# One core, four sublayers in fp32-by-splitting: half of the last block pair of each FFN computed plainly, and joined high/low activations for wider matmuls

## The chip, the core and the metric

The kernel runs on one core of a Trainium2 chip. Its time is the device time of one execution in microseconds (us), as the median of several runs. TensorE (PE) multiplies, VectorE (DVE) and ScalarE (ACT) prepare and collect operands, GpSimd (POOL) does a few elementwise steps and issues some transfers, and SyncE (SP) issues the weight transfers.

## The reference

The input is 256 tokens of width 2048 in float32. There are two layers. Each has a mixer and a dense FFN, both between RMS norms:

```python
for layer in range(DEPTH):                      # DEPTH = 2
    h = rms_norm(x, g[0])
    # layer 0: proj = h @ even_w_in;  GLA (8 heads) and neighbourhood attention (8 heads)
    # layer 1: proj = h @ odd_w_in;   SSD (16 heads) and sliding-window attention (8 heads)
    mix = concat(o_a, o_b) @ w_out
    x = x + rms_norm(mix, g[1])
    h = rms_norm(x, g[2])
    f = (silu(h @ w_gate) * (h @ w_up)) @ w_down   # hidden width 5632 = 11 blocks of 512
    x = x + rms_norm(f, g[3])
```

All weights are float32 and are read from memory once. The result is float32.

## The kernel before

**Arithmetic.** Every float32 operand is split into a high part (a copy that ACT rounds to the fast fp32r format) and a low part (DVE subtracts the high part from the original). A product of two operands is three matmuls: high by high, high by low, low by high. Weights arrive in halves of 128 x 1024 values (512 KB). `halves` (L179) makes `whi` on ACT (L184) and `wlo` on DVE (L186) of each half. Seven buffers of `whi` and seven of `wlo` rotate.

**Two kinds of projection.** `unit_a` (L198) has the activations stationary and 512 weight columns moving: lines L211 to L213, 512 columns each. `unit_b` (L233) has a weight tile of 128 x 128 stationary and the 256 tokens moving: lines L242 to L244, 256 columns each, 16 steps of three matmuls. The even layer uses `unit_b` for 24 weight chunks (queries and keys of both mixers) and for one narrow chunk of 48 used rows (kind "L"); the odd layer uses it for 12 chunks and for one narrow chunk. Activations after a norm are kept as eight tiles of 4 KB per partition, four `xth` and four `xtl` (L315).

**The FFN.** Ten of the eleven hidden blocks are taken in five pairs. While gate and up of a pair are computed, the down projection of the pair before runs in the background (`quads`, L555), half of the output columns at a time (`p` = 0, 1). One such half multiplies a 2 x 2 block matrix by a 2 x 2 block matrix with seven products instead of eight. That needs sums of weight tiles (`sw`, L567, DVE), sums of activations (`combos`, L528), 14 splits of weights (L184, L186), and ten additions of results into `f` and `fu` (L627). The products are lines L618 to L620 into the tile `sq`. Block 10 (`LONE`) has no partner: its gate and up run while the last pair's `quads` finish, and its down projection ends the FFN with a plain `unit_a` in `post` (L513).

**What sets the order.** The code is written as a main stream of projections. Background generators are advanced by `tick` at a given `rate`. A scheduler then orders the instructions of each engine, ahead of time, and allots tiles from pools. Each engine executes its own list in order. `self.tight` makes `unit_a` alternate between the two token halves after each weight half. At the end of `post`, lines pinned in order interleave the next norm with the last matmuls. There `x`, the residual, is loaded again from memory by POOL's queue (`load_x`, L631), added to the normed result (L413 on DVE, L411 on POOL), and transposed on PE.

**Tiles.** The general pool `s4` has 26 slots of 4 KB per partition. It holds the activations, the weight tiles of `quads`, the mixers' work, `f` and `x`.

Of the kernel before, what the change touches and what calls it, by code (L numbers as in the profile page):

```python
# [18 lines left out]
F32 = mybir.dt.float32  # L19
# [7 lines left out]
P = 128  # L27
# [8 lines left out]
PAIRS = [(0, 1), (2, 3), (4, 5), (6, 7), (8, 9)]  # L36
LONE = 10
# [7 lines left out]
NCHUNK = 298  # L45
NQUAD = 80
AHEAD, SETTLE = 2, 4
LAG = 2
# [43 lines left out]
class Trunk:  # L92
    def __init__(self, tc, dr, out, stage=99):
        self.tc, self.nc, self.dr, self.out, self.stage = tc, tc.nc, dr, out, stage
        self.plan = []
        self.pending = deque()
        self.bg = []
        self.early = deque()
        self.hooks, self.mid = deque(), deque()
        self.lag = 2 * LAG  # L100
        self.nraw = 0
        self.rate, self.width, self.credit = 1.0, 3, 0.0
        self.n = 0
        self.pinned = {}
        self.pinning = ()
        self.ready = deque()
        self.tight = False
        self.splan, self.sraw, self.squeue = [], {}, deque()
# [52 lines left out]
    def chunk(self, kind, name, idx, k0, n0):  # L161

        if self.hooks and len(self.plan) == self.hooks[0][0]:
            self.hooks.popleft()[1]()
        self.plan.append((kind, name, idx, k0, n0))
        while len(self.ready) < 2:
            self.prep()
        n = 2 if kind == "A" else 8
        return [tuple(v.rearrange("p (k n) -> p k n", k=n) for v in self.ready.popleft()) for _ in range(2)]

    def prep(self):

        while len(self.early) < 4 and self.nraw < 2 * NCHUNK:
            self.load_half()
        if not self.early:
            return
        self.ready.append(self.halves(self.early.popleft()))
# [20 lines left out]
    def unit_a(self, chunks, xk, evac):  # L198
# [21 lines left out]
        for ci, (name, idx, k0, n0, kt0) in enumerate(chunks):  # L220
            w = self.chunk("A", name, idx, k0, n0)
            if self.tight:
                for half in range(2):
                    part(0, ci, w, kt0, half)
                    part(1, ci, w, kt0, half)
                continue
# [4 lines left out]
            self.push(*(lambda h=h, ci=ci, w=w, kt0=kt0: part(1, ci, w, kt0, h) for h in range(2)))  # L231

# [72 lines left out]
    def begin_norm(self, li, gi):  # L305

        nc = self.nc
        xt = ([None] * 4, [None] * 4)
# [4 lines left out]
        def piece(t, j, src):  # L313
            if xt[0][j] is None:
                xt[0][j], xt[1][j] = self.slot([P, 4, T], F32R, "xth"), self.slot([P, 4, T], F32R, "xtl")  # L315
# [33 lines left out]
    def post(self, li, gi, nseg, after, f=None):  # L349
# [9 lines left out]

        def seg(mk, xk):  # L360
# [3 lines left out]
            if last:  # L364
                self.x = [[None, None], [None, None]]
                for t in range(2):
                    for j in range(2):
                        self.load_x(t, j, nc.gpsimd)
# [48 lines left out]
            for n in range(4):  # L417
                def evac(t, ps, n=n):
# [13 lines left out]
                    if n == 3 and t == 0:  # L432
# [3 lines left out]
                        self.pinning = ("PE", "DVE")  # L436
                if last and n == 2:
                    self.pinned = {}
                    self.pinning = ("PE",)
                self.unit_a(mk(n), xk, evac)  # L440
# [11 lines left out]
    def ffn(self, li, norm, after):  # L452
# [21 lines left out]
        for pi, pair in enumerate(PAIRS):  # L474
            self.squeue.extend((li, b, n) for p in range(2) for b, n in (
                (pair[0], 2 * p), (pair[0], 2 * p + 1), (pair[1], 2 * p + 1), (pair[1], 2 * p)))
        for pi, pair in enumerate(PAIRS):
# [14 lines left out]
            self.spawn(self.quads(li, pair, self.combos(h), f, pi == 0))  # L492
# [5 lines left out]
        self.rate = 2.0  # L498
        gate_up(LONE, whole)
        while self.bg:  # L500
            self.step()
        for n in range(4):
            u = f[2][:, n // 2 * 512:n // 2 * 512 + 512]
            c = slice(n % 2 * 512, n % 2 * 512 + 512)
            for t in range(2):
                d = f[t][n // 2][:, c]
                if n % 2 == 0 and t:
                    nc.vector.tensor_add(d, d, u)
                if n % 2:
                    nc.vector.tensor_sub(d, d, u)  # L510
        self.tight = False
        seg = self.post(li, 3, 1, after, f[:2])
        seg(lambda n: [("ffn_w_down", li, 512 * LONE, 512 * n, 0)], self.xk(ht))  # L513

# [13 lines left out]
    def combos(self, h):  # L528
# [4 lines left out]
        def put(key, src):  # L533
            o = self.slot([P, 2, 4, P], F32R, "so")
            nc.scalar.copy(o[:, 0], src)
            nc.vector.tensor_sub(o[:, 1], src, o[:, 0].bitcast(F32))  # L536
            out[key] = o
# [14 lines left out]
        put("t3", k)  # L552
        return out

    def quads(self, li, pair, ops, f, first):  # L555
# [4 lines left out]
        for p in range(2):  # L560
# [48 lines left out]
            for key in order:  # L609
                ps = self.mx([P, 512], "sq")  # L610
                x = ops[key]
                for i in range(2):
                    next(ahead, None)
                    wh, wl = (v.rearrange("p (k n) -> p k n", k=2) for v in ready.popleft())
                    for k in range(2):
                        s, e = i == 0 and k == 0, i == 1 and k == 1
                        xh, xl = x[:, 0, 2 * i + k], x[:, 1, 2 * i + k]
# [36 lines left out]
    def setup(self, ctx):  # L654
# [8 lines left out]
        self.s4 = pool("s4", 26)  # L663
# [61 lines left out]
    def even_mixers(self, norm, after):  # L725
# [18 lines left out]
        ps = self.unit_b(w, 0, 3072, xt, "L")  # L744
        nc.vector.tensor_mul(lrT, ps[0:48], row[0:48])
        for half in range(2):
            self.spawn(self.gla(half, lrT, mix))
        for half in range(2):
            t = self.slot([P, 2, 2, T], nm="gqk")
            for j in range(2):  # L750
                c0 = (2 * half + j) * P
                self.mul_row(t[:, 1, j], self.unit_b(w, 0, 512 + c0, xt), row)
                self.mul_row(t[:, 0, j], self.unit_b(w, 0, c0, xt), row, 0.125)
# [4 lines left out]
        for u in range(2):  # L758
            nq, nk = self.slot([P, 4, T], nm="nq"), self.slot([P, 4, T], nm="nk")
            for h in range(4):  # L760
                c0 = (4 * u + h) * P
                back = lambda x: x.rearrange("p (a t) -> p a t", a=2)[:, :, ::-1]
                self.mul_row(nq[:, h].rearrange("p (a t) -> p a t", a=2), back(self.unit_b(w, 0, 3104 + c0, xt)),
                             back(row), P ** -0.5)
                self.mul_row(nk[:, h], self.unit_b(w, 0, 4128 + c0, xt), row)
# [245 lines left out]
    def odd_mixers(self, norm, after):  # L1011
# [23 lines left out]
        ps = self.unit_b(w, 0, 2560, xt, "L")  # L1035
        self.spawn(self.ssd_dt(ps, row))
# [74 lines left out]
    def ssd_dt(self, ps, row):  # L1111
# [7 lines left out]
        xu = tl("dx")  # L1119
        x, u = xu[:, 0], xu[:, 1]  # L1120
        nc.vector.tensor_mul(x, ps[0:R], row[0:R])
# [289 lines left out]
```

## Time and profile before

| | |
|---|---|
| median of 3 runs | 2223.72 us (2223.66 to 2224.74) |
| the profiled execution's own time | 2221.77 us |
| its span | 2220.0 us |
| mean granted TensorE clock | 0.992 |
| busy: PE, DVE, ACT, POOL | 98%, 80%, 55%, 9% of the span |
| first FFN's last stage (block 10 and what follows) | about 1043 to 1151 us |
| second FFN's last stage | about 2096 to 2204 us |

How to read it: the span runs from the first to the last instruction of one execution. A matmul is shown from its start to its modelled end, so neighbours overlap; what one costs is the distance from its start to the next start. In a timeline row the bracket gives how long the engine sat idle before it and what ended that. A row of the windows view gives, for a stretch of time, the busy time and the number of instructions of each engine, then the granted clock.

### The profile page before, as it was taken

Reading aid. Unit: us, or ns where it says so; the run is one execution under the profiler, and the core shown is the slowest. Engines: PE = TensorE matmul, PEld = TensorE weight load, DVE = VectorE, ACT = ScalarE, POOL = GpSimd, SP = SyncE. Lnnn points to the kernel's source line nnn. Section 1 sums busy time; section 2 is a strip of 40 time slices with the busy share of each in tenths; the row PEclk is TensorE's granted clock in tenths of the full one; section 3 lists DMA queues with packets and bytes.
Section 4 is the critical chain, followed back from the end, with each engine's and each line's share of the span. In section 5 each row is a group of like instructions: output and inputs, shape, how many; then the busy total and the mean of one; then the engine's idle time right before and its main releaser. Section 6 shows DMA issues by size and latency. Waiting matters only on the chain.

```text
span 2220.0 us, 28963 instructions
## 1 busy us (share of the span) xinstructions
PE 2173.3 (98%) x10840; PEld 1829.0 (82%) x10840; DVE 1772.4 (80%) x2137; ACT 1213.5 (55%) x1515; POOL 205.3 (9%) x246
## 2 busy tenths in 40 slices
PE   8999999999999999999989999999999999999997
PEld 7989998788888888888768988878888888888875
DVE  7987545766878898888989988676687889888896
ACT  7544435555565555555656545655555555555563
POOL 0001010210000000000021362121000000000002
PEclk9999999999999999999999999999999999999998
DMA  8445565574665555465556443657466555646563
GB/s 282 133 133 184 182 203 182 180 258 157 204 234 189 204 178 201 159 217 199 204 188 223 158 144 114 224 187 260 158 201 229 198 204 170 202 165 209 199 216 116
DMA packets 117325, 424.54 MB, mean 191 GB/s; under 512 B 13392, under 2 KB 13520, under 8 KB 117184
## 3 DMA queue, kind: packets, MB, share of 16 engines
q1 hardware_dynamic: 110592, 400.61, 53.6%
q0 software_dynamic: 6448, 21.99, 3.0%
q8 instruction: 85, 1.39, 0.2%
q14 instruction: 56, 0.46, 0.1%
q10 hardware_dynamic: 144, 0.10, 0.0%
HBM read 414.25 MB, written 8.39 MB: 190 GB/s over the span
## 4 chain that ended last, share of the span: by engine, by line
PE 86%; DVE 10%; issue 2%; POOL 1%; DMA 1%; ACT 0%; DVEq 0%; POOLq 0%; ACTq 0%
PE acc L213 19%; PE acc L212 19%; PE acc L211 19%; DVE wlo L186 5%; PE sq L618 5%; PE sq L619 5%; PE sq L620 5%; PE accb L242 3%; PE accb L244 3%; PE accb L243 3%; PE tp L285 1%; DVE sw L567 1%; DVE xtl L331 1%; DVE f L627 1%; PE gs L819 1%
## 5 line engine op out<-in xcount | busy, mean ns | idle before, releaser
L186 DVE TENSOR_TENSOR wlo<-raw,whi 128x1024 fp32r<-128x1024 f32 x596 | 740.0, 1249 | 278.0 <-ACT whi L184 270.7
L184 ACT CAST whi<-raw 128x1024 fp32r<-128x1024 f32 x596 | 624.7, 1052 | 572.1 <-PE acc L213 388.7
L213 PE MATMUL acc<-whi,xtl 128*128 128x512 f32 x1760 | 689.7, 393 | 5.9 <-DVE xtl L331 5.9
L212 PE MATMUL acc<-wlo,xth 128*128 128x512 f32 x1760 | 689.3, 393 | 0.8 <-DVE wlo L186 0.8
L211 PE MATMUL acc<-whi,xth 128*128 128x512 f32 x1760 | 677.4, 393 | 3.1 <-ACT xth L328 3.0
L184 ACT CAST whi<-sw 128x1024 fp32r<-128x1024 f32 x280 | 293.7, 1054 | 232.0 <-PE acc L213 131.0
L213 PEld LDWEIGHTS acc<-whi,xtl 128*128 128x128 f32 x1760 | 332.4, 189 | 78.1 <-DVE xtl L331 9.3
L211 PEld LDWEIGHTS acc<-whi,xth 128*128 128x128 f32 x1760 | 332.3, 189 | 73.0 <-ACT xth L328 5.1
L212 PEld LDWEIGHTS acc<-wlo,xth 128*128 128x128 f32 x1760 | 332.4, 189 | 70.4 <-DVE wlo L186 1.7
L186 DVE TENSOR_TENSOR wlo<-sw,whi 128x1024 fp32r<-128x1024 f32 x280 | 338.2, 1222 | 48.9 <-ACT whi L184 46.0
L619 PE MATMUL sq<-wlo,so 128*128 128x512 f32 x560 | 220.0, 393 | 4.5 <-DVE wlo L186 4.5
L620 PE MATMUL sq<-whi,so 128*128 128x512 f32 x560 | 219.4, 392 | 0.0
L618 PE MATMUL sq<-whi,so 128*128 128x512 f32 x560 | 219.0, 393 | 0.0
L567 DVE TENSOR_TENSOR sw<-sw,sw 128x1024 f32<-128x1024 f32 x160 | 194.1, 1221 | 16.8 <-DMA sw<-sstream 16.3
L242 PE MATMUL accb<-xth,whi 128*128 128x256 f32 x608 | 173.8, 286 | 0.0
L244 PE MATMUL accb<-xth,wlo 128*128 128x256 f32 x608 | 173.0, 284 | 0.0
L243 PE MATMUL accb<-xtl,whi 128*128 128x256 f32 x608 | 172.7, 284 | 0.0
L619 PEld LDWEIGHTS sq<-wlo,so 128*128 128x128 f32 x560 | 105.9, 189 | 28.5 <-DVE wlo L186 7.0
L620 PEld LDWEIGHTS sq<-whi,so 128*128 128x128 f32 x560 | 106.0, 189 | 22.5 <-DVE so L536 0.6
L618 PEld LDWEIGHTS sq<-whi,so 128*128 128x128 f32 x560 | 105.8, 189 | 22.1 <-ACT whi L184 0.4
L635 POOL DMA_DIRECT2D x<-xm x8 | 4.4, 546 | 1292.5 <-ACT whi L184 645.6
L242 PEld LDWEIGHTS accb<-xth,whi 128*128 128x128 f32 x608 | 116.5, 192 | 1.4 <-issue 0.7
(248 smaller groups left out, 2226.9 us busy)
## 6 DMA issues: line engine op xcount, KB each, us to landing
raw<-wstream SPq DMA_DIRECT2D x596, 512.0 KB, 4.9
sw<-sstream SPq DMA_DIRECT2D x160, 512.0 KB, 6.2
gb<-norm_gains POOLq DMA_DIRECT2D x16, 256.0 KB, 7.6
xm<-x POOLq DMA_DIRECT2D x16, 256.0 KB, 3.5
x<-xm POOLq DMA_DIRECT2D x8, 512.0 KB, 5.1
x<-x SPq DMA_DIRECT2D x4, 512.0 KB, 8.2
x<-x POOLq DMA_DIRECT2D x4, 512.0 KB, 7.8
xf<-x POOLq DMA_DIRECT2D x8, 256.0 KB, 3.4
```

The lines of the kernel that those rows point to most:

```text
L184: self.pin(nc.scalar.copy(hi, src))
L186: self.pin(nc.vector.tensor_sub(lo, src, hi.bitcast(F32)))
L211: self.pin(nc.tensor.matmul(ps[t], xh, wh[:, k % 2], start=s, stop=False))
L212: self.pin(nc.tensor.matmul(ps[t], xh, wl[:, k % 2], start=False, stop=False))
L213: self.pin(nc.tensor.matmul(ps[t], xl, wh[:, k % 2], start=False, stop=e))
L242: nc.tensor.matmul(ps, wh[:, kt % 8], xh, start=kt == 0, stop=False)
L243: nc.tensor.matmul(ps, wh[:, kt % 8], xl, start=False, stop=False)
L244: nc.tensor.matmul(ps, wl[:, kt % 8], xh, start=False, stop=kt == 15)
L567: nc.vector.tensor_add(a, a, b)
L618: nc.tensor.matmul(ps, xh, wh[:, k], start=s, stop=False)
L619: nc.tensor.matmul(ps, xh, wl[:, k], start=False, stop=False)
L620: nc.tensor.matmul(ps, xl, wh[:, k], start=False, stop=e)
```

## The change

**Plain half.** For the last pair (blocks 8 and 9), `quads` runs only for `p` = 1 (`COLS`). The other half of the output columns (n = 0, 1) is computed plainly at the end: `post` gets three chunks for n = 0 and n = 1 (blocks 8, 9, 10) and one chunk for n = 2 and n = 3. The plain chunks use operands that `combos` makes anyway, and one more, `a21`. Eight weight tiles of 1 MB move from the stream for `quads` to the main stream (`NQUAD` 80 to 72, `NCHUNK` 298 to 306). The rate of the background work during block 10 goes from 2.0 to 0.75, so `quads` reaches into the final projection; it is drained before n = 2. The corrections with `fu` and the reloading of `x` move into the hook `before`.

**Joined activations.** After a norm, high and low parts lie in one 8 KB tile (pool `s8`, 4 slots; `s4` goes to 18). `unit_b2` replaces `unit_b` for the 24 chunks of the even layer: per step one matmul of 512 columns (high weight by both parts) and one of 256 (low weight by the high part), and at the end ACT copies one half of the result and DVE adds the other. `unit_l` takes the narrow chunks of both layers with one matmul of 512 columns per step: `lhalf` puts the low weights into unused columns of the high tile, so there is no `wlo` for them. It ends with two ACT copies and two DVE additions.

PE's list early in the even layer, before; `accb` is the result of one `unit_b`, `xth` and `xtl` the two parts of the activations:

```order
L243 MATMUL accb_474<-xtl_116,whi_464 128x256
L244 MATMUL accb_474<-xth_115,wlo_466 128x256
L242 MATMUL accb_474<-xth_115,whi_464 128x256
L243 MATMUL accb_474<-xtl_116,whi_464 128x256
L244 MATMUL accb_474<-xth_115,wlo_466 128x256
```

The same place in the changed kernel; `xt` is the joined tile, `acc_94` the result of one `unit_b2`:

```order
L263 MATMUL acc_94_444<-xt_118,wlo_436 128x256
L260 MATMUL acc_94_444<-xt_118,whi_434 128x512
L263 MATMUL acc_94_444<-xt_118,wlo_436 128x256
L260 MATMUL acc_94_444<-xt_118,whi_434 128x512
L263 MATMUL acc_94_444<-xt_118,wlo_436 128x256
```

Two matmuls of 256 columns with the same weights have become one of 512.

DVE's list in the first FFN's last stage, before: the second half of the last pair is being prepared while block 10 is computed (`sw` are sums of weight tiles, `sq` results of products, `raw` weights of block 10).

```order
L627 TENSOR_TENSOR f_4271<-f_4271,sq_9366 128x512
L567 TENSOR_TENSOR sw_9241<-sw_9241,sw_9314 128x1024
L567 TENSOR_TENSOR sw_9242<-sw_9242,sw_9315 128x1024
L508 TENSOR_TENSOR f_4271<-f_4271,fu_4273 128x512
L567 TENSOR_TENSOR sw_9314<-sw_9314,sw_9336 128x1024
L186 TENSOR_TENSOR wlo_9406<-sw_9241,whi_9404 128x1024
L567 TENSOR_TENSOR sw_9315<-sw_9315,sw_9337 128x1024
L627 TENSOR_TENSOR f_4270<-f_4270,sq_9401 128x512
L627 TENSOR_TENSOR fu_4273<-fu_4273,sq_9401 128x512
L186 TENSOR_TENSOR wlo_9422<-sw_9242,whi_9420 128x1024
```

DVE's list in the changed kernel at the end of block 10's gate and up (`h` is the hidden activation):

```order
L201 TENSOR_TENSOR wlo_9129<-raw_8989,whi_9127 128x1024
L201 TENSOR_TENSOR wlo_9135<-raw_9034,whi_9133 128x1024
L201 TENSOR_TENSOR wlo_9160<-sw_9017,whi_9158 128x1024
L533 SCALAR_TENSOR_TENSOR h_9075<-acc_8883,nrs_3801,sg_8849 128x512
L533 SCALAR_TENSOR_TENSOR h_9090<-acc_8890,nrs_3954,sg_8857 128x512
L201 TENSOR_TENSOR wlo_9178<-raw_9040,whi_9176 128x1024
L711 TENSOR_TENSOR f_3924<-f_3924,sq_9058 128x512
L201 TENSOR_TENSOR wlo_9184<-raw_9125,whi_9182 128x1024
```

Of the first half's sums, splits and additions nothing is left on DVE; in their place stand splits of plain weights (`raw_9040`, `raw_9125`), now behind `h`. From the first sum of activations of the last pair to the low part of block 10's activations DVE's list has 56 instructions of 1024 elements per partition and 38 shorter ones before, and 32 and 22 in the changed kernel.

POOL's list at the end of the first FFN, before (`gb` are gains, `x` the residual, `xm` its copy in memory, `f` the sums of the down projection):

```order
L635 DMA x_9704<-xm_147 128x1024
L635 DMA x_9706<-xm_147 128x1024
L635 DMA x_9708<-xm_148 128x1024
L635 DMA x_9710<-xm_148 128x1024
L371 DMA gb_9712<-norm_gains 128x512
L371 DMA gb_9714<-norm_gains 128x512
```

And in the changed kernel:

```order
L492 TENSOR_TENSOR f_3923<-f_3923,gb_9114 128x512
L492 TENSOR_TENSOR f_3925<-f_3925,gb_9114 128x512
L492 TENSOR_TENSOR f_3923<-f_3923,gb_9116 128x512
L719 DMA x_9409<-xm_148 128x1024
L719 DMA x_9411<-xm_148 128x1024
L719 DMA x_9413<-xm_149 128x1024
L719 DMA x_9415<-xm_149 128x1024
```

The four loads of `x` have moved behind three multiplications, the third of which needs the first token half of n = 1.

The diff, cut to its core:

```diff
+COLS = [(0, 1)] * 4 + [(1,)]
-NCHUNK = 298
-NQUAD = 80
+NCHUNK = 306
+NQUAD = 72
+LHALF = (9, 10, 331, 332)
+ENDRATE = .75
...
+    def lhalf(self, src):
+        nc = self.nc
+        with self.tc.high_priority(offset=PREP):
+            hi = self.whi.tile([P, 1024], F32R, tag="whi", name=self.nm("whi"))
+            self.pin(nc.scalar.copy(hi, src))
+            k, r = (v.rearrange("p (k n) -> p k n", k=8) for v in (hi, src))
+            self.pin(nc.vector.tensor_sub(k[:, :, 64:112], r[:, :, 0:48], k[:, :, 0:48].bitcast(F32)))
+        return hi, hi
...
-            if self.tight:
+            if self.tight and (loose is None or ci < loose):
...
+    def unit_b2(self, name, n0, xt):
+        nc = self.nc
+        self.flush()
+        w = self.chunk("B", name, 0, 0, n0)
+        ps = self.pacc.tile([P, 2, T], F32, tag="acc", name=self.nm("acc2"))
+        for kt in range(16):
+            wh, wl = w[kt // 8]
+            wide = lambda s, e: nc.tensor.matmul(ps, wh[:, kt % 8], self.joined(kt, xt), start=s, stop=e)
+            if kt < 15:
+                wide(kt == 0, False)
+            nc.tensor.matmul(ps[:, 0], wl[:, kt % 8], xt[0][kt // 4][:, kt % 4, :], start=False, stop=False)
+            if kt == 15:
+                wide(False, True)
+            if kt % 8 == 7:
+                self.tick()
+        t = self.tmp([P, T], nm="half")
+        nc.scalar.copy(t, ps[:, 1])
+        nc.vector.tensor_add(t, ps[:, 0], t)
+        return t
...
+    def unit_l(self, name, n0, xt, out, row):
...
+        for kt in range(16):
+            nc.tensor.matmul(ps, w[kt // 8][0][:, kt % 8], self.joined(kt, xt), start=kt == 0, stop=kt == 15)
...
+        nc.scalar.copy(t[:, 0], ps[0:48, 1])
+        nc.scalar.copy(t[:, 1], ps[64:112, 0])
+        nc.vector.tensor_add(t[:, 0], ps[0:48, 0], t[:, 0])
+        nc.vector.tensor_add(t[:, 0], t[:, 0], t[:, 1])
...
-                xt[0][j], xt[1][j] = self.slot([P, 4, T], F32R, "xth"), self.slot([P, 4, T], F32R, "xtl")
+                xt[2][j] = self.s8.tile([P, 2, 4, T], F32R, tag="s8", name=self.nm("xt"))
+                xt[0][j], xt[1][j] = xt[2][j][:, 0], xt[2][j][:, 1]
...
+                if before is not None:
+                    before(n)
+                    if n == 2:
+                        reload()
...
-        self.rate = 2.0
+        def before(n):
+            if n == 2:
+                while self.bg:
+                    self.step()
+                self.tight = False
+            if n % 2 == 0:
+                u = f[2][:, n // 2 * 512:n // 2 * 512 + 512]
...
+        self.rate = ENDRATE
         gate_up(LONE, whole)
-        while self.bg:
-            self.step()
...
-        seg(lambda n: [("ffn_w_down", li, 512 * LONE, 512 * n, 0)], self.xk(ht))
+        own = [(b, 4 * i) for i, b in enumerate((*PAIRS[-1], LONE))]
+        seg(lambda n: [("ffn_w_down", li, 512 * b, 512 * n, k) for b, k in (own[2:] if n > 1 else own)], operand)
...
-        self.s4 = pool("s4", 26)
+        self.s4 = pool("s4", 18)
+        self.s8 = pool("s8", 4)
```

102 lines of the change are left out of this document (61 added, 41 removed).

## The prediction

> **What bounds the kernel now.** I read the page first, then the windows view by stage, then the timeline where the windows differ.
>
> ```profile
> span 2220.0 us, 28963 instructions
> PE 2173.3 (98%) x10840; PEld 1829.0 (82%) x10840; DVE 1772.4 (80%) x2137; ACT 1213.5 (55%) x1515; POOL 205.3 (9%) x246
> PE 86%; DVE 10%; issue 2%; POOL 1%; DMA 1%; ACT 0%; DVEq 0%; POOLq 0%; ACTq 0%
> ```
>
> PE sets the end nearly everywhere; DVE has a tenth of the chain. The windows say where: a quiet stretch of 75 us, then the same length in the last stage of each FFN.
>
> ```profile
> core 0: us, PE busy (x) PEld busy (x) DVE busy (x) ACT busy (x) POOL busy (x), PEclk, DMA share, GB/s
> 900.00:975.00 75.00, 75.00 (x337) 62.20 (x336) 63.80 (x67) 41.52 (x46) 0.00 (x0) 1.00 0.57 191
> 1059.00:1134.00 75.00, 69.22 (x292) 55.98 (x292) 73.16 (x77) 41.41 (x45) 4.30 (x8) 0.95 0.68 232
> 2112.00:2187.00 75.00, 68.25 (x293) 54.77 (x293) 72.86 (x77) 41.41 (x45) 4.30 (x8) 0.98 0.65 218
> ```
>
> In both FFN stretches DVE is busy 73 of 75 us and PE gets through 45 and 44 matmuls fewer. Busy time hides part of that, so I go by counts. What one matmul costs, from start to start:
>
> ```profile
> 699.71 0.39 PE L211 MATMUL acc<-whi,xth 128*128 128x512 f32 x1
> ...
> 701.98 0.39 PE L619 MATMUL sq<-wlo,so 128*128 128x512 f32 x1
> ```
> ```profile
> 200.09 0.28 PE L244 MATMUL accb<-xth,wlo 128*128 128x256 f32 x1
> ...
> 201.29 0.28 PE L242 MATMUL accb<-xth,whi 128*128 128x256 f32 x1
> ```
>
> Ten steps of 512 columns take 2.27 us, 0.227 each; ten of 256 take 1.20 us, 0.120 each. The 45 and 44 missing matmuls are 10.2 and 10.0 us. The timeline names the waits:
>
> ```profile
> 1094.60 0.50 PE L619 MATMUL sq<-wlo,so 128*128 128x512 f32 x1 [1.81 <-DVE wlo L186]
> ...
> 1095.68 0.63 PE L619 MATMUL sq<-wlo,so 128*128 128x512 f32 x1
> 1096.11 0.63 PE L620 MATMUL sq<-whi,so 128*128 128x512 f32 x1
> ...
> 1127.91 0.66 PE L285 MATMUL tp<-ca,h 128*128 128x128 f32 x4 [3.51 <-DVE h L466]
> ```
> ```profile
> 2147.56 0.51 PE L619 MATMUL sq<-wlo,so 128*128 128x512 f32 x1 [1.81 <-DVE wlo L186]
> 2147.90 0.40 PE L620 MATMUL sq<-whi,so 128*128 128x512 f32 x1
> ...
> 2180.86 1.12 PE L285 MATMUL tp<-ca,h 128*128 128x128 f32 x4 [3.91 <-DVE h L466]
> ```
>
> PE waits for a low weight part, and at the end for `h`, which stands in DVE's queue behind all that is late. After the wait at 1094 the matmuls are 0.43 us apart for some 3 us: the clock was halved, and that is part of the 10.2.
> The Trainium skill ("TensorE: Matmul & The Clock Gate", Part 1) puts halving down to an idle window of about 3.4 us that runs freely. The trace agrees in part: an equal wait at 2147 was followed by steps of 0.23. It changes no term.
>
> **The last stage of an FFN: removed, added, moved.** DVE's cost per instruction, again from start to start:
>
> ```profile
> 1098.99 1.29 DVE L627 TENSOR_TENSOR f<-f,sq 128x512 f32<-128x512 f32 x2
> 1100.19 3.50 DVE L186 TENSOR_TENSOR wlo<-sw,whi 128x1024 fp32r<-128x1024 f32 x3
> 1103.60 1.23 DVE L567 TENSOR_TENSOR sw<-sw,sw 128x1024 f32<-128x1024 f32 x1
> ```
>
> Two additions of 512 take 1.20 us, 0.60 each; three splits take 3.41 us, 1.137 each; sums of weights cost the same. The plain half removes 14 splits, 8 sums and 10 additions on DVE per FFN and adds 8 splits and one split of activations (0.6): 6 x 1.137 + 8 x 1.137 + 10 x 0.60 - 0.6 = 21.3 us less. On PE 7 x 12 = 84 matmuls become 8 x 12 = 96: 12 x 0.227 = 2.7 us more. ACT loses six splits less one small copy, and at 41 of 75 us it has room.
>
> Does that clear the stall? I count instructions in the two orders, from the transposes of the last pair's `h` to the first matmul that needs block 10's activations. Before: 56 long instructions, 36 short ones and two `h` on DVE, 56 x 1.137 + 38 x 0.60 = 86.5 us, against 340 matmuls, 77.2 us. DVE is 9.3 us too slow, close to the 10 that are lost. Changed: 32 long and 22 short, 49.6 us, against 291 matmuls, 66.1 us. The tightest point inside is the third split of block 10's later weights: 9 long and 11 short rows, 16.8 us, with 101 matmuls, 22.9 us, before it is used; some 6 us to spare, of which ACT's copies of `h` take about one. `h` itself then stands behind no backlog. So the stall should go: -20.2 us over both FFNs. Nothing (if all work merely waits elsewhere) to -20.2 are the bounds; I take the whole, because the counts reproduce the stall of before.
>
> **The reloading of `x`.** Its four transfers move behind a multiplication on POOL that needs n = 1's first result.
>
> ```profile
> 1138.56 1.29 POOL L429 TENSOR_TENSOR f<-f,gb 128x512 f32<-128x512 f32 x1 [30.02 <-ACT sq L303]
> ```
> ```profile
> 1137.03 0.69 DVE L381 TENSOR_TENSOR f<-f,acc 128x512 f32<-128x512 f32 x1 [0.58 <-PE acc L213]
> ...
> 1147.17 0.68 DVE L381 TENSOR_TENSOR f<-f,acc 128x512 f32<-128x512 f32 x1
> ...
> 1150.41 1.10 DVE L413 SCALAR_TENSOR_TENSOR x<-f,prs,x 128x512 f32<-128x512 f32 x1
> ```
> ```profile
> x<-xm POOLq DMA_DIRECT2D x8, 512.0 KB, 5.1
> x<-x POOLq DMA_DIRECT2D x4, 512.0 KB, 7.8
> ```
>
> From DVE's addition (1137.03) to the end of POOL's multiplication (1139.85) are 2.8 us. The transfer then takes 5.1 us, or 7.8 like those of the other mixer: `x` is there 7.9 to 10.6 us after n = 1's addition. It is wanted 24 matmuls (5.4 us) plus the 3.2 us from the last addition (1147.17) to line 413 (1150.41), so 8.7 us after. In time by 0.8, or late by 1.9. What queues behind are PE's transposes and, in the second FFN, the end itself. I take 0.5 per FFN, +1.0, with 0 and +3.8 as bounds.
>
> **Joined activations.** 24 chunks: 16 steps of 0.227 + 0.120 = 0.347 instead of 3 x 0.120 = 0.360 save 384 x 0.013 = 5.0 us. The two narrow chunks: 16 x 0.227 = 3.6 instead of 48 x 0.120 = 5.8 save 4.3 together. Added: 24 copies on ACT and 24 additions on DVE of 256 columns, nearest rows:
>
> ```profile
> L1106 ACT ACTIVATE xs<-xsT 128x256 f32<-128x256 f32 x8 | 3.1, 383 | 7.3 <-PE xsT L1105 7.3
> ```
> ```profile
> L690 DVE TENSOR_TENSOR nk<-accb,rstdB 128x256 f32<-128x256 f32 x8 | 3.4, 424 | 4.4 <-PE accb L244 4.3
> ```
> ```profile
> 40.00:120.00 80.00, 80.00 (x622) 72.11 (x621) 67.29 (x102) 45.12 (x52) 0.00 (x0) 1.00 0.45 148
> ...
> 200.00:320.00 120.00, 120.00 (x870) 114.28 (x869) 64.51 (x101) 48.94 (x66) 15.75 (x20) 1.00 0.61 193
> ```
>
> Sixteen of them fall where DVE and ACT have half their time free; eight in the tighter first window: 8 x 0.424 = 3.4 us into 12.7 free. I cost them at nothing; uncovered they would be 24 x 0.81 = 19 us. The narrow chunks also drop four splits. The smaller general pool reorders the mixers' side work a little; its price has no row here, from -4 (odd stage waits gone) to +4, taken as 0.
>
> **Sum.** Profiled execution 2221.77 - 20.2 (stalls) + 5.4 (24 more matmuls) - 5.0 - 4.3 (joined) + 1.0 (`x`) = 2198.7. The median of the runs lies 1.95 above that execution, so 2200.6.
>
> **Rivals.**
> 1. *DVE's lateness becomes another wait.* The chain copy on ACT, sum on DVE, split on ACT, split on DVE starts the last half, and ACT's list is strict; if it eats the 6 us to spare, half the stall stays: +10.1, 2210.7. Against: 49.6 us of DVE work in 66.
> 2. *`x` late.* Both FFNs at 1.9 us: +2.8 on the forecast, 2203.4; with slow transfers 2206.
> 3. *Joining halves saves nothing*: a matmul costs its columns alone, a joined one 2 x 0.120 = 0.240. Then the 24 chunks save nothing and the narrow ones 2 x (5.76 - 3.84) = 3.8: 5.5 more, 2206.1. Against it stands 0.227 in the row above. The Trainium skill ("TensorE: Matmul & The Clock Gate", Back-to-back issue gap) speaks for it: columns over 2.4 GHz plus 2.5 ns, which leaves 2.5 ns to save where the rows here show 13. The measurement decides.
> 4. *Slower: weight loads exposed.* If a narrow matmul behind a joined one cannot hide its weight load, each of 384 pairs pays what is paid after a switch:
>
> ```profile
> 267.87 0.47 PE L242 MATMUL accb<-xth,whi 128*128 128x256 f32 x1
> 268.18 0.28 PE L243 MATMUL accb<-xtl,whi 128*128 128x256 f32 x1
> ```
>
> 0.31 instead of 0.12, so 0.19 x 384 = 73 us: 2274. It decides from 23.1 / 384 = 0.06 us per pair. Against: loads hide behind 256 columns now, and a joined matmul gives them longer.
> 5. *The plain half clears nothing*, because the stalls have another cause: 2223.7 - 3.9 + 1.0 = 2220.8, no change that can be told.
>
> **How the numbers follow.** Forecast 64%, within 2196 to 2206 (the bounds for `x` and the pool). Rival 1 15%, rival 2 8%, rival 3 5%, rival 4 3%, rival 5 5%. The range, 2194 to 2212, takes in the forecast and rivals 1 to 3. A measurement here tells 0.2%, 4.4 us, from no change. Faster: forecast and rivals 1 to 3, 92%; same: rival 5, 5%; slower: 3%.
>
> **What would show it.** In the changed profile the windows of the last stages should hold as many matmuls as a quiet one, with no bracket naming `wlo` or `h`, and DVE near 75% there. Wide steps should start 0.227 apart and narrow ones 0.120. At line 476 a DMA as releaser would mean `x` is late. Waits of over 5 us left in these stages, pairs over 0.36 us, or new waits in the odd mixer would make the prediction wrong.

## The result and the profile after

The changed kernel takes 2202.06 us (median of 4 runs, 2201.54 to 2202.50) against 2224.15 us before (2223.66 to 2224.74): 0.990 of the time, 95% interval 0.9883 to 0.9918. Forecast were 2200.6 us and a range of 2194 to 2212. The profiled execution took 2202.50 us and has a span of 2200.6 us, 19.4 less than before. That this span equals the forecast, which is a time of a run and not a span, is chance.

The head of the page after, and its chain of waits by engine:

```profile
span 2200.6 us, 28141 instructions
PE 2163.8 (98%) x10416; PEld 1804.1 (82%) x10416; DVE 1741.3 (79%) x2119; ACT 1212.2 (55%) x1533; POOL 212.9 (10%) x246
PE 92%; DVE 4%; issue 2%; ACT 1%; POOL 1%; DMA 0%; DVEq 0%; SPq 0%; POOLq 0%; ACTq 0%
```

VectorE's share of the chain fell from 10% to 4%, although its busy share hardly moved. The windows view says where: again the quiet stretch and the last stage of each FFN (columns as in the prediction).

```profile
core 0: us, PE busy (x) PEld busy (x) DVE busy (x) ACT busy (x) POOL busy (x), PEclk, DMA share, GB/s
900.00:975.00 75.00, 75.00 (x340) 62.29 (x340) 68.08 (x73) 42.27 (x47) 0.00 (x0) 1.00 0.57 196
...
1060.00:1135.00 75.00, 75.00 (x336) 62.20 (x336) 56.13 (x57) 37.46 (x43) 8.10 (x8) 1.00 0.59 188
...
2110.00:2185.00 75.00, 75.00 (x337) 62.19 (x336) 53.74 (x58) 34.65 (x42) 10.34 (x10) 1.00 0.48 159
```

TensorE is busy for all 75 us of both and gets through 336 and 337 matmuls, 4 and 3 fewer than in the quiet stretch; before, 45 and 44 were missing. VectorE went from 73 us of work to 56 and 54. The changed stages end earlier; in the stretches that lie as far from their ends as those of before (1046 to 1121 and 2095 to 2170 us) TensorE gets through 336 matmuls as well, with VectorE at 63 us. No bracket in the timeline names a low weight part or `h` between 1040 and 1135 us.

To compare the stages I take the first transpose of `x` in each norm (first and last start are the two times behind the durations). Before, then after; the view is that of the transposes of a window:

```profile
L285 PE MATMUL tp<-ca,x x8: 272/272/328, 427.8 to 430.0; 128*128 128x128 f32 x8
L285 PE MATMUL tp<-ca,x x4: 272/272/328, 1151.6 to 1151.9; 128*128 128x128 f32 x4
L285 PE MATMUL tp<-ca,x x4: 272/272/299, 1482.7 to 1483.0; 128*128 128x128 f32 x4
```
```profile
L343 PE MATMUL tp<-ca,x x16: 272/273/329, 424.1 to 430.2; 128*128 128x128 f32 x16
L343 PE MATMUL tp<-ca,x x16: 270/272/328, 1138.8 to 1145.2; 128*128 128x128 f32 x16
L343 PE MATMUL tp<-ca,x x16: 270/272/302, 1471.0 to 1478.4; 128*128 128x128 f32 x16
```

The differences of these marks, and of the last one to the end of the span, are the four stages. The other kernels of the study, read in the same way from one profiled execution each:

| us | even mixer | FFN 0 | odd mixer | FFN 1 to the end | median of its runs | before, same chip |
|---|---|---|---|---|---|---|
| before | 427.8 | 723.8 | 331.1 | 737.3 | 2224.15 | |
| the change | 424.1 | 714.7 | 332.2 | 729.6 | 2202.06 | 2224.15 |
| plain_only | 428.7 | 716.0 | 330.2 | 729.6 | 2207.12 | 2223.20 |
| joined_only | 423.0 | 722.5 | 335.3 | 736.5 | 2221.39 | 2223.20 |
| pool_only | 429.7 | 723.5 | 332.1 | 737.7 | 2223.32 | 2223.20 |
| grouped | 421.6 | 714.7 | 333.2 | 729.5 | 2201.51 | 2223.20 |
| fewer_splits_4 | 429.1 | 719.2 | 331.2 | 732.8 | 2214.58 | 2222.22 |
| fewer_splits_14 | 429.3 | 716.4 | 332.8 | 731.3 | 2211.19 | 2222.22 |
| rate_2 | 423.9 | 717.3 | 332.2 | 732.5 | 2207.60 | 2222.22 |
| x_earlier | 424.2 | 715.0 | 333.1 | 729.8 | 2203.35 | 2222.22 |
| odd_narrow_back | 423.9 | 714.7 | 331.8 | 729.7 | 2201.49 | 2225.02 |
| odd_back_grouped | 423.0 | 715.0 | 331.7 | 730.1 | 2200.45 | 2225.02 |
| odd_pace_95 | 422.9 | 714.8 | 336.6 | 729.9 | 2204.20 | 2225.02 |
| odd_pace_85 | 422.5 | 714.7 | 332.2 | 729.6 | 2200.83 | 2225.02 |

So the change gained 3.7, 9.1 and 7.7 us in the even mixer and the two FFNs and lost 1.1 in the odd mixer. The seven kernels with the change's FFN behind joined activations (x_earlier moves only its loads) lie within 0.3 us of each other in FFN 0 (714.7 to 715.0) and within 0.6 in FFN 1 (729.5 to 730.1). The mixers move by 1 to 2 us between executions. Part of that comes from short drops of TensorE's granted clock (last section), which cost some 1.5 us each and fall in some executions and not in others. So a difference of 1 to 2 us between two mixers in this table shows little by itself.

### The profile page after: what moved, and what is told of

It is laid out like the page before. It is cut to its first block, busy times and chain, and to the rows that moved or that the text cites. A ratio compares the mean times of both kernels' runs of the same rounds, so it can differ in the third digit from the quotient of the medians.

```text
span 2200.6 us, 28141 instructions
## 1 busy us (share of the span) xinstructions
PE 2163.8 (98%) x10416; PEld 1804.1 (82%) x10416; DVE 1741.3 (79%) x2119; ACT 1212.2 (55%) x1533; POOL 212.9 (10%) x246
## 4 chain that ended last, share of the span: by engine, by line
PE 92%; DVE 4%; issue 2%; ACT 1%; POOL 1%; DMA 0%; DVEq 0%; SPq 0%; POOLq 0%; ACTq 0%
PE acc L229 21%; PE acc L227 21%; PE acc L228 21%; PE sq L703 5%; PE sq L702 5%; PE sq L704 5%; PE acc L260 4%; PE acc L263 2%; DVE wlo L201 2%; PE tp L343 1%; DVE xt L390 1%; PE gs L903 1%; PE accb L300 1%; PE accb L301 1%; PE accb L302 1%
## 5 line engine op out<-in xcount | busy, mean ns | idle before, releaser
L229 PE MATMUL acc<-whi,xt 128*128 128x512 f32 x1760 | 689.2, 392 | 7.9 <-DVE xt L390 7.9
L228 PE MATMUL acc<-wlo,xt 128*128 128x512 f32 x1760 | 686.9, 391 | 0.0
L227 PE MATMUL acc<-whi,xt 128*128 128x512 f32 x1760 | 678.8, 392 | 4.2 <-ACT xt L387 3.2
L229 PEld LDWEIGHTS acc<-whi,xt 128*128 128x128 f32 x1760 | 331.4, 188 | 79.8 <-DVE xt L390 11.1
L227 PEld LDWEIGHTS acc<-whi,xt 128*128 128x128 f32 x1760 | 331.6, 188 | 73.8 <-ACT xt L387 5.3
L228 PEld LDWEIGHTS acc<-wlo,xt 128*128 128x128 f32 x1760 | 331.4, 188 | 69.3 <-DVE wlo L201 0.8
L201 DVE TENSOR_TENSOR wlo<-sw,whi 128x1024 fp32r<-128x1024 f32 x252 | 305.5, 1221 | 55.4 <-ACT whi L199 52.3
L704 PE MATMUL sq<-whi,so 128*128 128x512 f32 x504 | 196.1, 389 | 0.0
L702 PE MATMUL sq<-whi,so 128*128 128x512 f32 x504 | 195.8, 390 | 0.0
L260 PE MATMUL acc<-xt,whi 128*128 128x512 f32 x384 | 138.0, 404 | 0.0
L702 PEld LDWEIGHTS sq<-whi,so 128*128 128x128 f32 x504 | 94.6, 188 | 19.4
L703 PEld LDWEIGHTS sq<-wlo,so 128*128 128x128 f32 x504 | 94.6, 188 | 19.4
L263 PE MATMUL acc<-xt,wlo 128*128 128x256 f32 x384 | 105.8, 286 | 0.0
L227 PE MATMUL acc<-whi,mixh 128*128 128x512 f32 x256 | 98.5, 396 | 0.6 <-ACT sz L788 0.6
L229 PE MATMUL acc<-whi,mixl 128*128 128x512 f32 x256 | 97.9, 391 | 0.0
```

What stands on the lines that cost most here:

```text
L201: self.pin(nc.vector.tensor_sub(lo, src, hi.bitcast(F32)))
L227: self.pin(nc.tensor.matmul(ps[t], xh, wh[:, k % 2], start=s, stop=False))
L228: self.pin(nc.tensor.matmul(ps[t], xh, wl[:, k % 2], start=False, stop=False))
L229: self.pin(nc.tensor.matmul(ps[t], xl, wh[:, k % 2], start=False, stop=e))
L260: wide = lambda s, e: nc.tensor.matmul(ps, wh[:, kt % 8], self.joined(kt, xt), start=s, stop=e)
L263: nc.tensor.matmul(ps[:, 0], wl[:, kt % 8], xt[0][kt // 4][:, kt % 4, :], start=False, stop=False)
```

## The experiments

**The plain half alone.** The change with all of the joining undone.

```diff
-        self.s4 = pool("s4", 18)
-        self.s8 = pool("s8", 4)
+        self.s4 = pool("s4", 26)
-        self.unit_l(w, 3072, xt, lrT, row)
+        ps = self.unit_b(w, 0, 3072, xt, "L")
...  (unit_b for unit_b2 everywhere, LHALF empty)
```

> The plain half of each FFN's last pair alone: activations separate in 26 slots of 4 KB, every narrow projection again three 256-column matmuls, the narrow chunk again split in full. Theory (both FFN stalls go, and 24 matmuls per FFN part are paid for): 2224.15 - 20.2 + 5.4 = 2209.4 us. Rival (the odd mixer's waits, which are 4.6 us longer in the changed kernel, grew because the FFN ahead of it is arranged differently): the same plus 4.6, 2214.0. If the plain half cleared nothing: 2229.6.

Measured: 2207.12 us, 0.9925 of before (0.9908 to 0.9941), 16.1 less. The FFN stages fell by 7.8 and 7.7 us; with the 12 added matmuls of each (2.7 us) that is 10.5 and 10.4 us of stall gone, against the 10.1 each of the prediction. The odd mixer did not grow, it lost 0.9, and its waits are those of the kernel before (1.47 and 0.83 us for the tile `seg`), so the rival that blamed the FFN's arrangement for the odd mixer's waits falls.

**Joining alone.** The change with the last pair's seven products for both column halves again.

```diff
-COLS = [(0, 1)] * 4 + [(1,)]
+COLS = [(0, 1)] * 5
-ENDRATE = .75
+ENDRATE = 2.0
...  (post, combos and the end of ffn as before; NCHUNK 298, NQUAD 80)
```

> The joined activations alone (24 joined chunks, both narrow chunks, 18 slots of 4 KB and 4 of 8 KB), with the last pair's seven products for both column halves as before. By the prediction's terms: -5.0 - 4.3 = -9.3, 2214.9 us. By the pairs as they are spaced in the changed kernel's trace (0.352 us instead of 0.347) and the 1.6 us that its clock lost near 57 us: 384 x 0.008 + 4.3 - 1.6 = 5.8 less, 2218.4. If the smaller general pool is what lengthens the odd mixer's waits: 4.6 more, 2223.0.

Measured: 2221.39 us, 0.9983 (0.9974 to 0.9992), only 1.8 less; its ten runs spread from 2216.5 to 2222.7. The stages of the profiled execution (2219.14 us) say where: 4.8 less in the even mixer, 4.2 more in the odd one, whose only changes are the narrow chunk and the pools. In part this is that execution: one wait is 1.97 us there and 0.81 at the same matmul of the change, and the granted clock is 0.66 in the 5 us behind it (1395 to 1400 us), where the change has 1.00. The third expectation comes nearest in time, but blames the pool:

**The pools alone.** An edit of the kernel before.

```diff
-                xt[0][j], xt[1][j] = self.slot([P, 4, T], F32R, "xth"), self.slot([P, 4, T], F32R, "xtl")
+                x2 = self.s8.tile([P, 2, 4, T], F32R, tag="s8", name=self.nm("xt"))
+                xt[0][j], xt[1][j] = x2[:, 0], x2[:, 1]
-        self.s4 = pool("s4", 26)
+        self.s4 = pool("s4", 18)
+        self.s8 = pool("s8", 4)
```

> The kernel before with only the memory of the change: the two parts of the split activations lie in one 8 KB tile of a pool of their own, and the general pool has 18 slots instead of 26; every matmul is the one of before. Theory (the pool costs nothing): 2224.15 us. Rival (fewer free slots lengthen the odd mixer's waits by the 4.6 us seen after the change): 2228.8, with the 4.6 us between 1300 and 1420 us.

Measured: 2223.32 us against 2223.20, ratio 1.000 (0.9991 to 1.001). No cost of the pool shows. The odd mixer is 1.0 us longer in this one execution, but its waits are those of before (1.48 and 0.83 us for `seg`), and behind them the granted clock drops to 0.71 (1308 to 1313 us, 17 matmuls), where the kernel before has 1.00 (1307 to 1312 us, 23 matmuls).

**Wide and narrow matmuls in groups.** An edit of the change.

```diff
-        for kt in range(16):
-            ...
-            if kt < 15:
-                wide(kt == 0, False)
-            nc.tensor.matmul(ps[:, 0], wl[:, kt % 8], ...)
+        for g in range(2):
+            ...
+            for k in range(8 - g):
+                wide(k)
+            for k in range(8):
+                low(k)
+            if g:
+                wide(7)
```

> The changed kernel with the matmuls of a joined chunk in another order: eight 512-column ones, then eight 256-column ones, twice, instead of one and one in turn. If the 5 ns that a pair takes over 0.347 us are paid at the change from wide to narrow, 384 changes become 48: 336 x 0.005 = 1.7 us less, 2200.4 us, pairs 0.347 on the mean. If they belong to the wide matmul as such: 2202.1. If narrow matmuls behind one another cannot hide their weight loads behind 256 columns: slower than 2204; the kernel before speaks against that, with 0.120 from start to start.

First the pairs of the change, in its timeline near 45 us:

```profile
45.20 0.40 PE L260 MATMUL acc<-xt,whi 128*128 128x512 f32 x1
45.44 0.28 PE L263 MATMUL acc<-xt,wlo 128*128 128x256 f32 x1
45.55 0.40 PE L260 MATMUL acc<-xt,whi 128*128 128x512 f32 x1
...
47.67 0.40 PE L260 MATMUL acc<-xt,whi 128*128 128x512 f32 x1
```

Seven pairs take 2.47 us, 0.353 each: 0.24 from wide to narrow and 0.11 back. Grouped:

```profile
44.35 2.23 PE L260 MATMUL acc<-xt,whi 128*128 128x512 f32 x9
46.41 1.12 PE L261 MATMUL acc<-xt,wlo 128*128 128x256 f32 x8
47.37 0.86 PE L260 MATMUL acc<-xt,whi 128*128 128x512 f32 x3
```

Nine wide ones take 2.06 us, 0.229 each, and eight narrow ones 0.96, 0.120 each: 0.349 for a wide and a narrow one, so of the 6 ns over 0.347 some 4 are paid at the changes. The four kernels with grouped chunks have a mean of 422.5 us in the even mixer, the five with joined chunks in turn 423.8; that is near the 1.7 expected, but three of those five executions (the change, rate_2, odd_narrow_back) have a clock drop of some 1.4 us in this stage and none of the four has. Without it some 0.5 us are left, so the gain of grouping by stages is not shown; by the spacing of the matmuls it is 4 ns for each of 384 pairs, 1.5 us. The median, 2201.51 us, is 0.55 under that of the change and too close to be told from it.

**VectorE's work in the last stage, taken away in doses.** In the kernel before, the first 4 or all 14 subtractions for low weight parts of the first column half of each FFN's last pair are left out. The matmuls that would read them read the high part, so TensorE's work and the transfers stay the same.

```diff
+            if not low:
+                return hi, hi
             lo = self.wlo.tile([P, 1024], F32R, tag="wlo", name=self.nm("wlo"))
...
-                        ready.append(self.halves(w[i]))
+                        ready.append(self.halves(w[i], pair != PAIRS[-1] or p == 1 or len(done) >= 4))
+                        done.append(0)
```

> The kernel before without the first 4 subtractions for low weight parts in the first column half of each FFN's last pair; the matmuls that would read them read the high part instead, so that the low parts of these weights are left out of the result and TensorE's work is unchanged. Theory (VectorE is 9.3 us late there by counts): 4 x 1.137 = 4.5 us less work and 4.5 us less stall in each FFN, 2224.15 - 9.1 = 2215.1 us. Rival (the stall has another cause): 2224.2.

> The same with all 14 subtractions of that column half left out: the low parts of all combined weights of the first column half of each FFN's last pair are missing from the result. Theory: 15.9 us less work for VectorE in each FFN, more than the 9.3 it is late, so the stall goes whole and no more: 2224.15 - 20.2 = 2204.0 us. If time goes on falling with VectorE's work: 2224.15 - 31.8 = 2192.4. Rival (another cause): 2224.2.

Measured: 2214.58 us (0.9961, 0.9946 to 0.9976) and 2211.19 us (0.9942, 0.9926 to 0.9959). With 4 left out the FFN stages fell by 4.6 and 4.5 us, one for one with 4 x 1.137 = 4.5 us of work. With 14, they fell by 7.4 and 6.0 instead of 10.1. What is left is a wait for `h`, first with 4 and then with 14 subtractions left out:

```profile
1124.67 0.66 PE L287 MATMUL tp<-ca,h 128*128 128x128 f32 x4 [3.89 <-DVE h L468]
```
```profile
1123.66 0.66 PE L287 MATMUL tp<-ca,h 128*128 128x128 f32 x4 [2.75 <-DVE h L468]
```

And in the 50 us ahead of the second one (columns as above):

```profile
1075.00:1125.00 50.00, 47.25 (x211) 38.91 (x210) 49.91 (x54) 28.36 (x29) 4.30 (x8) 1.00 0.63 224
```

VectorE is busy for 49.91 of 50 us there although 15.9 us of its work are gone from the first column half: the second half's products and block 10 fill it by themselves. So the cause is VectorE's queue, and the theory's sum over the whole stage is too coarse: work taken away early doesn't help a stretch that is too full later. The plain half takes work from both ends: the second half's products are then spread over block 10 and what follows. What that spreading is worth, the next run shows.

**The pace of the products.** An edit of the change.

```diff
-ENDRATE = .75
+ENDRATE = 2.0
```

> The changed kernel with the pace of the products during block 10 back at 2 steps per half chunk instead of 0.75. The same instructions come in another order: by counts from the two orders VectorE's tightest point, a combined activation, falls 12.1 us further behind than in the changed kernel, which has some 6 us to spare. Theory: a stall of about 6 us in each FFN comes back, 2202.06 + 12 = 2214 us. Rival (only the total of VectorE's work counts): 2202.1.

Measured: 2207.60 us (0.9928, 0.9913 to 0.9943); the FFN stages grew by 2.6 and 2.9 us, 5.5 together. Its waits:

```profile
1052.65 0.50 PE L704 MATMUL sq<-whi,so 128*128 128x512 f32 x1 [0.48 <-DVE so L618]
1054.98 0.50 PE L703 MATMUL sq<-wlo,so 128*128 128x512 f32 x1 [0.45 <-DVE wlo L201]
1063.14 0.50 PE L703 MATMUL sq<-wlo,so 128*128 128x512 f32 x1 [0.55 <-DVE wlo L201]
```

The same instructions, bunched, bring a stall back, at the combined activations and low parts as expected, so the order matters beside the total. Only the size was off: if the queue falls 12.1 us further behind, as the expectation counts, and that costs 2.7, some 9.4 us were to spare and not 6; this is an estimate, by the same one-for-one rule that held for 4 subtractions and not for 14.

**`x` one column quarter earlier.** An edit of the change.

```diff
-                    if n == 2:
+                    if n == 1:
                         reload()
```

> The changed kernel with the reloading of x one column quarter earlier, ahead of n = 1 instead of n = 2. The prediction put 1.0 us on a late x; in the trace of the changed kernel no addition waits for its transfer. If x is in time there: 2202.1 us. If it is late by the predicted 0.5 per FFN: 2201.1; by the upper bound of 1.9 per FFN: 2198.3. If the tiles that x now claims earlier are missing elsewhere: over 2204.

Measured: 2203.35 us (0.991, 0.9895 to 0.9925), not faster: `x` was in time. In the trace of the change the view of line 476 names no transfer among what ended its idle time:

```profile
L476 DVE SCALAR_TENSOR_TENSOR x<-f,prs,x x18: 737/752/1780, 422.8 to 2192.9; 128x512 f32<-128x512 f32 x18
...
its engine sat idle before it (us, times) until:
  POOL prs L357: 2.0, 4
```

and that of the tile `x` around the first FFN's end, with the row of these loads in the list of transfers, has

```profile
L719 POOL DMA_DIRECT2D x<-xm x4: 537/537/577, 1131.7 to 1133.4; - x4
L476 DVE SCALAR_TENSOR_TENSOR x<-f,prs,x x4: 737/746/1020, 1137.7 to 1156.3; 128x512 f32<-128x512 f32 x4
```
```profile
x<-xm POOLq DMA_DIRECT2D x8, 512.0 KB, 5.9
```

The first transfer is issued 6.0 us before the first use, and the median load takes 5.9 us, inside the 5.1 to 7.8 of the prediction. So `x` was in time, but with little to spare: line 476 starts straight behind VectorE's instruction before it (at 1137.7 us), and it stands 1.1 us ahead of the first transpose of `x` both here and in x_earlier.

**The odd layer's narrow chunk undone.** The waits that are new in the odd mixer, in the timeline of the change:

```profile
1339.87 0.50 PE L227 MATMUL acc<-whi,xt 128*128 128x512 f32 x1 [0.94 <-ACT rq L1139]
1354.78 1.13 PE L1070 MATMUL apo<-pT,kw 128*128 128x256 f32 x4 [0.49 <-ACT pT L1066]
...
1383.35 1.10 PE L1070 MATMUL apo<-pT,kw 128*128 128x256 f32 x4 [1.27 <-DVE mxv L1039]
1385.98 1.13 PE L1070 MATMUL apo<-pT,kw 128*128 128x256 f32 x4 [0.81 <-ACT pT L1066]
```

TensorE waits for the attention heads' work, mostly the softmax, in places that it passed without a wait before. The kernel before has two waits there, 1.47 and 0.83 us for `seg`, 2.3 in all; the waits that the timeline of the change names, two short ones for `seg` among them, sum to 4.7 (both counted from 30 us into the stage, behind the norm's own waits). The joined narrow chunk itself comes early and is as short as forecast; its even twin:

```profile
35.19 3.79 PE L281 MATMUL accl<-xt,whi 128*128 128x512 f32 x16
38.82 0.39 PE L260 MATMUL acc<-xt,whi 128*128 128x512 f32 x1
```

16 steps in 3.63 us. The edit:

```diff
-LHALF = (9, 10, 331, 332)
+LHALF = (9, 10)
-        self.unit_l(w, 2560, xt, xu[:, 0], row)
+        ps = self.unit_b(w, 0, 2560, xt, "L")
+        nc.vector.tensor_mul(xu[:, 0], ps[0:48], row[0:48])
...
```

With it TensorE's order in the odd mixer is that of the kernel before again.

> The changed kernel with the odd layer's narrow chunk again as 48 matmuls of 256 columns and full splits; the even layer's stays joined. TensorE's order in the odd mixer is then the one of before. Theory (the joined narrow chunk saves 2.1 us itself, but the order that the scheduler builds behind it adds some 5.6 us of waits between 1330 and 1390 us): that stage takes the 330.2 us that it took with the plain half alone, up to 1.0 more with the smaller pool, instead of 332.2: 2200.1 to 2201.1 us. Rival (the waits come from the pool or from other edits): 2.1 us are lost, 2204.2.

Measured: 2201.49 us (0.9892, 0.9878 to 0.9907), 0.57 under the median of the change where the theory had 1.0 to 2.0 and the rival 2.1 more. The windows view of the stretch with the waits, the change and then this kernel:

```profile
1300.00:1400.00 100.00, 95.52 (x485) 79.49 (x483) 78.32 (x173) 56.76 (x109) 39.96 (x38) 1.00 0.40 133
```
```profile
1300.00:1400.00 100.00, 100.00 (x504) 84.59 (x503) 77.94 (x169) 61.07 (x116) 31.94 (x38) 1.00 0.40 133
```

The 4.5 us of idle TensorE there are gone, so those waits belong to the order that goes with the joined narrow chunk. But others are back earlier in the mixer:

```profile
1292.02 1.10 PE L1328 MATMUL yp<-xs,seg 128*128 128x64 f32 x8 [1.48 <-POOL seg L1322]
1293.95 1.10 PE L1328 MATMUL yp<-xs,seg 128*128 128x64 f32 x8 [0.83 <-POOL seg L1322]
```

and the chunk takes its 2.1 us more. Net, the stage is 331.8 instead of 332.2 us: joining the odd narrow chunk saves 2.1 and gives some 2.5 back in these two executions. Behind the second wait this one also has a clock drop (0.66, the third column from the end):

```profile
1294.00:1299.00 5.00, 5.00 (x19) 4.15 (x20) 3.50 (x11) 1.69 (x2) 1.26 (x2) 0.66 0.01 3
```

Eight matmuls there start 0.42 us apart instead of 0.23, which costs some 1.5 us; the change has no such drop between 1180 and 1450 us. Without it the stage would take some 330.3 us, what the theory said, and the joined chunk would give back about 4. The medians, 0.57 apart with intervals that overlap, don't decide between these.

**That with grouped chunks, and two other paces of the odd mixer's side work.** The first combines the last edit with the groups. The other two have the groups and the joined narrow chunk, so the run to compare them with is grouped (333.2 us, 2201.51 in all); here the one at .95:

```diff
-RATE1, WIDTH1 = .9, 6
+RATE1, WIDTH1 = .95, 6
```

> The same, with the joined chunks in groups of eight wide and eight narrow matmuls. If the two gains add (2.0 to 1.0 and the 0.5 by the medians of the earlier run, 1.7 by the spacing of the pairs): 2198.5 to 2200.5 us, the fastest so far. If not: 2201.5.

> The changed kernel with grouped chunks, the odd layer's narrow chunk joined, and the pace of the odd mixer's side work at 0.95 steps instead of 0.9, which orders it anew. If the waits belong to one arrangement and not to the narrow chunk itself, the odd mixer's stage moves by several us: from 328 (waits as before, 2.1 saved) to over 334; 2197 to 2204 us. If the narrow chunk itself makes its followers late, the stage stays at 333 within 1 us: 2201.5.

> The same at 0.85 steps: by the first reading the stage moves again, to another value between 328 and over 334 us; by the second it stays at 333 within 1 us, 2201.5 us in all.

Measured: 2200.45 us (0.9888, 0.9873 to 0.9903), 2204.20 us (0.9906, 0.9891 to 0.9921) and 2200.83 us (0.9892, 0.9875 to 0.9908). The odd mixer takes 336.6 us at a pace of 0.95, as the first reading has it, but 332.2 at 0.85, within 1 us of grouped's 333.2, as the second has it. So the two do not settle it by their times. In the timeline the waits move with the pace: at 0.85 there are three of 0.50 to 0.65 us for `seg`, where grouped has two of 0.21 and 0.29, and the longest, 1.52 us for `mxv`, is that of a matmul into `apt` instead of `apo`. But in all seven executions with the joined odd narrow chunk the waits named in this mixer sum to 4.1 to 5.9 us, and in all seven without it to 2.3. That the order brings the waits is shown; that another order with the joined chunk would be free of them is not, and neither pace reached the 328 us that one with the waits of before would have. The lowest median, 2200.45, is 1.6 us under that of the change, with intervals that overlap: no version here is shown to beat the change.

## Why the prediction was right

The mechanism that carries the sum, the stall behind VectorE, was right. That the total came so near is in part luck: smaller terms were wrong both ways. One thing that the prediction named as a sign against it, new waits in the odd mixer, did come.

- **Stalls of the FFNs' last stages, -20.2:** right. VectorE's queue was the cause (one for one with 4.5 us of work taken away), and plain_only shows 10.5 + 10.4 = 20.9 us gone. Rivals 1 and 5 fall: no wait of another engine took the stall's place in these stages. The counts that the argument used were coarser than it let on: the total over the stage had VectorE 9.3 us late, but 15.9 us less work at its beginning cleared only 7.4 and 6.0 us; and the "some 6 us to spare" are 9.4 by the estimate from rate_2.
- **24 more matmuls, +5.4:** the FFN stages are shorter by 9.1 and 7.7 us, against 10.1 - 2.7 = 7.4 each. The 1.7 extra in the first come mostly with the joining: plain_only lost 7.8 there, and joined_only alone 1.3. It lies at the stage's beginning: in its first 60 us TensorE starts 252 matmuls in the change, joined_only and grouped, and 247 before and in plain_only, 5 x 0.227 = 1.1 us. Which step of the norm does it is not shown.
- **24 joined chunks, -5.0:** right in kind, mis-sized. The sum took 0.227 + 0.120 from stretches of one width; in turn they cost 0.353, so 0.007 is saved instead of 0.013, 2.7 us. Over the whole even mixer, 284 uninterrupted pairs of the change (those under 0.45 us) have a mean of 0.353 and 369 triples of the kernel before 0.361, so 0.008 or 3.1 us. By stages: the five kernels with chunks joined in turn have a mean of 423.8 us in the even mixer, the five with separate parts 428.9; 5.1 less, of which 2.1 are the narrow chunk, leaves 3.0. Three executions of each five have the clock drop near 57 us, so it cancels here. Rival 3 (nothing saved) falls, though its price for a joined matmul, 0.240, is what one takes up to the narrow one behind it. Rival 4 (weight loads exposed) falls too: of the change's 297 uninterrupted pairs in the even mixer 281 are at most 0.36, and the rest are the five of the clock drop and scattered ones like those of the kernel before. The Trainium skill ("TensorE: Matmul & The Clock Gate", Back-to-back issue gap) would have left 2.5 ns to save where 7 were measured and 13 forecast.
- **Two narrow chunks, -4.3:** the chunk takes 3.63 us as forecast. The even one is a gain; the odd one's 2.1 us were given back by the order behind it.
- **`x` late, +1.0:** it was not late; the term is 0, its lower bound. Rival 2 falls. Its "with slow transfers 2206" had no working behind it: the 1.9 us of the line already took the 7.8 us transfer.
- **Pools and odd mixers, 0 (-4 to +4):** +1.1 measured in the odd mixer where -2.1 of the narrow chunk was forecast, so some +3 inside the bounds. The prediction gave this price to the smaller pool. The runs give it to the joined narrow chunk: with the pool alone, or with that chunk undone, the waits are those of before, 2.3 us, and with it they are 4.7 in another order. That the chunk's gain would be used up by the order behind it was not in the sum.

By stages, forecast and measured: even mixer -7.1 and -3.7, first FFN -7.4 and -9.1, odd mixer with `x` -1.6 and +1.1, second FFN with `x` -6.9 and -7.7. That is -23.1 against -19.4 in the profiled executions, with errors both ways. Of the 3.4 us that the even mixer lacks, 1.9 are the mis-sized pair (384 x 0.005) and 1.4 the clock drop near 57 us, which the profiled execution of before doesn't have. The medians are 22.1 apart. The difference lies in the executions that were profiled: the one before is 2.38 us under its median of 2224.15 (1.95 under that of the three runs that the forecast had), the one after 0.44 over. For the profiled execution the forecast was 2198.7 us and 2202.50 were measured, 3.8 more; that it is within 1.5 us of the median is luck in part.

By medians the two halves alone give 16.1 + 1.8 = 17.9 us and together 22.1. In the profiled executions the odd mixer has 3.1 of these 4.2 (335.3 us with joining alone, 332.2 with both), most of it the longer wait and the clock drop told above. Whether these also set the medians is not shown: the ten runs of joining alone spread over 6.2 us, and the medians of before differ by up to 2.8 from chip to chip.

## What to carry to other kernels

An engine with spare time on the average can still set the end in one stage: compare its instructions with those of the bounding engine between two points of that stage, and do it at each use, since work taken away early doesn't empty a queue that overflows later. Price a mixed sequence of matmuls from a mixed sequence, not from runs of equal ones; nearly half of a small gain can lie in that. An edit that shortens one step by 2 us can have a scheduler order a whole stage anew, and what this costs can be as large as the gain: such edits need a run of their own. Before two stages of single executions are compared, compare their granted clocks in short windows: one drop here costs some 1.5 us, where the joined narrow chunk saves 2.1.

## What was not expected of the hardware

TensorE's clock dropped for some 3 us near 57 us, in some executions and not in others. The window 56 to 61 us of the change and of x_earlier, whose programs are alike up to the first FFN's end (the third column from the end is the granted clock):

```profile
56.00:61.00 5.00, 5.00 (x19) 4.04 (x20) 2.49 (x4) 4.88 (x7) 0.00 (x0) 0.66 0.22 73
```
```profile
56.00:61.00 5.00, 5.00 (x26) 3.93 (x26) 2.44 (x6) 4.87 (x7) 0.00 (x0) 1.00 0.32 105
```

TensorE counts as busy for all 5 us in both. In the first its pairs are 0.64 us apart instead of 0.353:

```profile
57.17 0.63 PE L260 MATMUL acc<-xt,whi 128*128 128x512 f32 x1
57.60 0.41 PE L263 MATMUL acc<-xt,wlo 128*128 128x256 f32 x1
57.81 0.63 PE L260 MATMUL acc<-xt,whi 128*128 128x512 f32 x1
```

Five slow pairs cost 5 x 0.29 = 1.4 us. pool_only and both kernels with fewer splits have a clock under 1 there too, with separate activations, so it does not come from joining. What stands just ahead are matmuls of 16 partitions (`gz`), a few at a time among the others; whether these bring it on was not tried. Such drops stand elsewhere too, with or without a visible wait ahead: behind the two waits for `seg` in the odd mixer, in the seven kernels with the order of before, the clock drops in four executions (pool_only, fewer_splits_14, odd_narrow_back, odd_back_grouped) and not in the other three.
